# Attention's modulation summed by TensorE, scores two heads ahead, the last tiles by halves, and long matmuls first in the up projections

## The chip, the cores and the metric

One core of one Trainium2 chip. The metric is device time in microseconds (us) of the whole kernel; lower is better.

## The reference, cut to what matters

256 tokens of width 1024 pass through ten phases: attention, an MLP, a recurrent block, an MLP, and then twice a gated feed-forward, a mixer and another gated feed-forward. The change touches the first phase, and one helper that the MLPs and the gated feed-forwards share.

```python
mod = silu(c) @ w + b                      # 1024 x 3072; shift, scale, gate
h = x * (1.0 + scale) + shift
q, k, v = split(h @ w_in)                  # 8 query heads, 2 key and value heads of 128
q, k = partial_rope(q), partial_rope(k)    # the first 32 of 128 are rotated
scores = where(|qpos - kpos| <= 128, q . k * 128**-0.5, -inf)
m = max(max(scores), sink)
probs = exp(scores - m) / (sum(exp(scores - m)) + exp(sink - m))
y = concat(probs @ v) @ w_out
x = layer_norm(2**0.5 * x + (1.0 + gate) * y)
# later: square(relu(h @ w1)) @ w2 (d_ff 4096), and (silu(h @ wg) * (h @ wu)) @ w2 (d_ff 2816)
```

## The kernel before

Weights come as a stream of 128x2048 f32 tiles (1 MB, `raw<-wst`, three slots), each holding two work items in the order of `items_of`. A call of `get` loads up to three tiles ahead on SP's queue and splits items up to four ahead: ScalarE writes the high half `hi` (fp32r, L357), VectorE the low half `lo` = raw - hi (L361). An item in `RAW` or at a phase's head is used unsplit. A product of split operands is three matmuls (hi by hi, low of the activations by hi, high of them by lo): `up_mm` (L385 to L387) and `mv_mm` (L422 to L424). `up_wide`, used by MLPs and feed-forwards alone, puts the first two in one matmul of 512 columns (high and low halves of `hT` side by side, L396) and the third in one of 256 (L397), and alternates the two eight times for one 128-column tile of weights.

Before the phases, the attention's shift and scale are made. `ada0` lies in sixteen chunks of 128x1024 (two halves of eight); VectorE multiplies each by `silu(c)` and adds it up (`mac`, L474 and L476), TensorE sums over partitions with a column of ones (L1560), and ScalarE applies the result to the transposed x (`feature`, L1564, into `hf`); then ScalarE and VectorE split it into `hT` (L374, L376). The two key heads are projected from `hf` unsplit (L411).

Attention (`ph_attn`) then makes v, q of heads 0 and 1, and in a loop over heads: q of head h + 2 with its rotation (`qk`: copy L702, shuffle L704, GpSimd's multiplication L705, VectorE's L706 and L707), the output projection of head h - 2 into four accumulators (two halves of the rows by two halves of the columns, `Down`), the transposes of the probabilities of head h (L737), the scores of h + 1 (L714, with mask, maximum, exponentials and sum in L718 to L729), and the values of h (L746). The last four heads' output tiles are kept back and added in `finish`, half by half, followed by the layer norm (`ln_stats`, L586 to L604), the transposes of x (`turn`, L613) and the first four items of the next phase (L636). Beside this, tasks from the list `side` load and add up the next modulations in VectorE (`aw<-adaw`, L476, closed by `ada_sum`, L490 to L499); `get` takes some of them at each call. A scheduler orders each engine's instructions from this code by dependencies and priorities; every engine, and SP's and GpSimd's DMA queues, then run strictly in that order.

## Time and profile before

| | us |
|---|---|
| median of 3 timed runs | 2131.32 (2127.93 to 2136.0) |
| the profiled execution | 2126.86 |
| its span, first to last instruction | 2125.1 |
| TensorE busy | 2042.1 (96%) |
| VectorE busy | 1568.1 (74%) |
| ScalarE busy | 1112.1 (52%) |
| GpSimd busy | 151.3 (7%) |

The profile is of one execution. An engine's busy time counts the spans of its instructions once; matmuls are pipelined and their ends are modelled, so the rate of matmuls is read from start to start. "Idle before" is the time an engine stood still ahead of an instruction, and the arrow names what ended it. PEclk is the granted share of TensorE's 2.4 GHz.

### The profile page before, as it was taken

To read this page: it belongs to the slowest core of one execution; us is meant where nothing else is said; L and a number is where in the kernel's file an instruction comes from. 1 tells how busy PE (TensorE), PEld (TensorE's weight loads), DVE (VectorE), ACT (ScalarE), POOL (GpSimd) and SP (SyncE) were. 2 spreads that over 40 slices of the span, in tenths; PEclk is the share of its full clock that TensorE was granted. 3 is DMA by queue.
4 is the path that set the end of the run, shared out by engine and by line. 5 is a ranking of instruction groups with operands and counts; after the bars stand their busy time and mean duration, and the time that the engine had idled before them with its cause. 6 is when DMAs were issued, how large, how long until landed. Compare 5 with 4: busy or idle time off the path is not lost.

```text
span 2125.1 us, 33174 instructions
## 1 busy us (share of the span) xinstructions
PE 2042.1 (96%) x13002; PEld 1798.5 (85%) x13002; DVE 1568.1 (74%) x2742; ACT 1112.1 (52%) x1964; POOL 151.3 (7%) x181
## 2 busy tenths in 40 slices
PE   4889999999999999999999999999999999999997
PEld 4778888898888888888999888888889889998886
DVE  5889989987766766689966666676668897667665
ACT  2454455784544555477634355545546774444552
POOL 1210000001010000012011000000001110100000
PEclk8999999999999999999999999999999999999999
DMA  9868884454664555454424465555545344355552
...
DMA packets 67803, 411.67 MB, mean 194 GB/s; under 512 B 8272, under 2 KB 8448, under 8 KB 26944
## 3 DMA queue, kind: packets, MB, share of 16 engines
...
q14 instruction: 53, 0.43, 0.1%
...
## 4 chain that ended last, share of the span: by engine, by line
PE 76%; DVE 13%; DMA 3%; ACT 3%; issue 2%; POOL 2%; POOLq 0%; DVEq 0%; SPq 0%; ACTq 0%
PE pu L396 19%; PE pu L397 10%; PE acc L422 6%; PE acc L423 6%; PE acc L424 6%; PE pu L385 3%; PE hd L636 3%; DVE lo L361 3%; PE pu L387 3%; PE pu L386 3%; DMA raw<-wst 2%; PE py L387 1%; PE py L385 1%; PE py L386 1%; DVE X L589 1%
## 5 line engine op out<-in xcount | busy, mean ns | idle before, releaser
L361 DVE TENSOR_TENSOR lo<-raw,hi 128x1024 fp32r<-128x1024 f32 (+1 forms) x689 | 731.4, 1071 | 313.2 <-ACT hi L357 300.1
L357 ACT ACTIVATE hi<-raw 128x1024 fp32r<-128x1024 f32 x574 | 605.0, 1057 | 548.1 <-PE pu L396 208.2
L396 PE MATMUL pu<-hT,hi 128*128 128x512 f32 x1760 | 625.5, 397 | 0.0
L397 PE MATMUL pu<-hT,lo 128*128 128x256 f32 x1760 | 493.3, 280 | 0.0
L396 PEld LDWEIGHTS pu<-hT,hi 128*128 128x128 f32 x1760 | 330.5, 188 | 80.1 <-ACT tT L374 0.4
L397 PEld LDWEIGHTS pu<-hT,lo 128*128 128x128 f32 x1760 | 332.2, 189 | 5.0
L422 PE MATMUL acc<-hi,tT 128*128 128x512 f32 x688 | 270.7, 395 | 2.3 <-ACT tT L374 2.3
L423 PE MATMUL acc<-hi,tT 128*128 128x512 f32 x688 | 271.1, 394 | 0.6 <-DVE tT L376 0.6
L424 PE MATMUL acc<-lo,tT 128*128 128x512 f32 x688 | 269.7, 392 | 0.0
L385 PE MATMUL pu<-hT,hi 128*128 128x256 f32 x896 | 261.5, 292 | 0.2 <-DVE sp L455 0.2
L387 PE MATMUL pu<-hT,lo 128*128 128x256 f32 x896 | 255.6, 285 | 4.0 <-DVE lo L361 4.0
L386 PE MATMUL pu<-hT,hi 128*128 128x256 f32 x896 | 255.6, 285 | 0.0
L385 PEld LDWEIGHTS pu<-hT,hi 128*128 128x128 f32 x896 | 172.6, 193 | 10.8 <-issue 9.7
L387 PEld LDWEIGHTS pu<-hT,lo 128*128 128x128 f32 x896 | 172.5, 193 | 4.3 <-DVE lo L361 4.2
L386 PEld LDWEIGHTS pu<-hT,hi 128*128 128x128 f32 x896 | 172.6, 193 | 1.2 <-issue 1.0
L422 PEld LDWEIGHTS acc<-hi,tT 128*128 128x128 f32 x688 | 129.0, 188 | 34.3 <-ACT tT L374 4.6
L424 PEld LDWEIGHTS acc<-lo,tT 128*128 128x128 f32 x688 | 129.3, 188 | 28.5 <-DVE lo L361 0.4
L423 PEld LDWEIGHTS acc<-hi,tT 128*128 128x128 f32 x688 | 129.2, 188 | 24.6 <-DVE tT L376 2.7
L636 PE MATMUL hd<-h,raw 128*128 128x128 f32 x960 | 113.2, 277 | 0.1
L636 PEld LDWEIGHTS hd<-h,raw 128*128 128x128 f32 x960 | 110.4, 193 | 2.4 <-ACT h L615 1.5
L405 DVE TENSOR_TENSOR u<-pu,u 128x256 f32<-128x256 f32 x140 | 59.0, 422 | 66.9 <-ACT u L404 66.8
L476 DVE SCALAR_TENSOR_TENSOR aacc<-aw,csil,aacc 128x1024 f32<-128x1024 f32 x70 | 89.3, 1276 | 0.9 <-DMA aw<-adaw 0.8
...
## 6 DMA issues: line engine op xcount, KB each, us to landing
raw<-wst SPq DMA_DIRECT2D x318, 1024.0 KB, 4.9
...
```

The lines of the kernel that those rows point to most:

```text
L357: S.activation(out=hi[:, 0:n], in_=r, func=AF.Copy)
L361: V.tensor_tensor(out=lo[:, c:c + m], in0=r[:, c:c + m], in1=hi[:, c:c + m].bitcast(F32), op=ALU.subtract)
L385: T.matmul(ps, lhsT=hi[:, c], rhs=r[:, 0:256], start=kk == 0, stop=False)
L386: T.matmul(ps, lhsT=hi[:, c], rhs=r[:, 256:512], start=False, stop=False)
L387: T.matmul(ps, lhsT=lo[:, c], rhs=r[:, 0:256], start=False, stop=kk == KT - 1)
L396: T.matmul(ps, lhsT=hi[:, c], rhs=r, start=kk == 0, stop=False)
L397: T.matmul(ps[:, 0:256], lhsT=lo[:, c], rhs=r[:, 0:256], start=False, stop=kk == KT - 1)
L422: T.matmul(ps, lhsT=th, rhs=hi, start=first, stop=False)
L423: T.matmul(ps, lhsT=tl, rhs=hi, start=False, stop=False)
L424: T.matmul(ps, lhsT=th, rhs=lo, start=False, stop=last)
L476: V.scalar_tensor_tensor(out=acc, in0=w, scalar=csil[:, k:k + 1], in1=acc, op0=ALU.mult, op1=ALU.add)
L636: T.matmul(ps[:, half * 128:half * 128 + 128], lhsT=w[:, kk * 128:kk * 128 + 128], rhs=h32[:, kk, :], start=kk == 0, stop=kk == KT - 1)
```

## The change

Modulation: the chunks get six slots of their own. `silu(c)` is spread over 32 columns (`csr`), and each chunk is four matmuls with it, one for each quarter of the chunk's columns, into the four 32-row groups of one PSUM tile (`chunk_mm`). When eight are summed, ScalarE copies the tile, TensorE transposes it in two pieces and VectorE adds the bias (`sums`). The second half's chunks alternate with the key matmuls of the first. The splits into `hT` are written after all keys. On the queues, sinks, mask and rotary table go from GpSimd's to SP's, behind the chunks and three weight tiles.

Attention: q of heads 0 and 1 come before v, the scores of a head two turns ahead of its transposes, the values one turn later. All rotary multiplications are VectorE's, and `nsk` is GpSimd's. The side tasks are to end two items earlier. The last heads' output tiles are added for the first half of the rows before the second.

`up_wide` issues its eight matmuls of 512 columns first and then the eight of 256. `ln_stats` runs through its steps for one half of the columns and then for the other.

```diff
@@ items_of
-        out = [("k", 0), ("k", 1), ("v", 0), ("v", 1), ("q", 0), ("q", 1)]
+        out = [("k", 0), ("k", 1), ("q", 0), ("q", 1), ("v", 0), ("v", 1)]
@@ fused_kernel
-    nc.gpsimd.dma_start(out=vc, in_=vecs.broadcast_to([128, NV]))
...
@@ fetch, get
+    def fetch(n):
+        while ws["dma"] < min(len(st) // 2, n):
             u = ws["dma"]
             raws[u] = pw.tile([128, 2048], F32, tag="raw", bufs=3, name="raw")
             nc.sync.dma_start(out=raws[u], in_=wst[u])
             ws["dma"] += 1
+
+    def get(*key):
+        i = ws["cur"]
+        assert st[i] == key, (st[i], key)
+        fetch(i // 2 + ws["ahead"])
...
-            left = max(1, sum(1 for k in st[i:] if k[0] == key[0]) - (3 if key[0] == "attn" else 20))
+            left = max(1, sum(1 for k in st[i:] if k[0] == key[0]) - (5 if key[0] == "attn" else 20))
@@ up_wide
         hi, lo = w
         for kk in range(KT):
-            c = slice(kk * 128, kk * 128 + 128)
-            r = rhs(kk)
-            T.matmul(ps, lhsT=hi[:, c], rhs=r, start=kk == 0, stop=False)
-            T.matmul(ps[:, 0:256], lhsT=lo[:, c], rhs=r[:, 0:256], start=False, stop=kk == KT - 1)
+            T.matmul(ps, lhsT=hi[:, kk * 128:kk * 128 + 128], rhs=rhs(kk), start=kk == 0, stop=False)
+        for kk in range(KT):
+            T.matmul(ps[:, 0:256], lhsT=lo[:, kk * 128:kk * 128 + 128], rhs=rhs(kk)[:, 0:256], start=False, stop=kk == KT - 1)
 
@@ ln_stats
-        if ln["g1"] is not None:
-            for c, s in enumerate(cs_):
+        for c, s in enumerate(cs_):
+            if ln["g1"] is not None:
                 t = pool.tile([128, 512], F32, tag="t1", bufs=2, name="t1")
                 V.tensor_tensor(out=t, in0=src[c], in1=ln["g1"][:, s], op=ALU.mult)
                 src[c] = t
-        for c, s in enumerate(cs_):
             V.scalar_tensor_tensor(out=X[half][:, s], in0=X[half][:, s], scalar=SQ2, in1=src[c], op0=ALU.mult, op1=ALU.add)
-        for c, s in enumerate(cs_):
             V.bn_stats(out=stt[:, c, :], in_=X[half][:, s])
@@ finish
-                for j, (t, (hi, lo)) in enumerate(tail):
-                    mv_mm(acc[half, c], t, half, hi[:, c * 512:c * 512 + 512], lo[:, c * 512:c * 512 + 512], False, j == n - 1)
+                for j, (t, (hi, lo)) in enumerate(tails[half]):
+                    mv_mm(acc[half, c], t, half, hi[:, c * 512:c * 512 + 512], lo[:, c * 512:c * 512 + 512], False, j == len(tails[half]) - 1)
@@ Down
-                self.tail.append((t, w))
+                for half in range(2):
+                    self.tail[half].append((t, w))
             else:
                 for half in range(2):
-                    for c in range(2):
-                        s = slice(c * 512, c * 512 + 512)
-                        if isinstance(w, tuple):
-                            mv_mm(self.acc[half, c], t, half, w[0][:, s], w[1][:, s], self.k == 0, False)
-                        else:
-                            T.matmul(self.acc[half, c], lhsT=t[:, half * 128:half * 128 + 128], rhs=w[:, s], start=self.k == 0, stop=False)
+                    self.part(half, t, w, self.k == 0)
             self.k += 1
+
+        def part(self, half, t, w, first=False):
+
+            for c in range(2):
+                s = slice(c * 512, c * 512 + 512)
+                mv_mm(self.acc[half, c], t, half, w[0][:, s], w[1][:, s], first, False)
@@ ph_attn
-        V.tensor_scalar(out=nsk, in0=vc[:, 0:8], scalar1=-1.0, scalar2=None, op0=ALU.mult)
-        E1, E2 = G, V
+        G.tensor_scalar(out=nsk, in0=vc[:, 0:8], scalar1=-1.0, scalar2=None, op0=ALU.mult)
...
-            E1.tensor_tensor(out=sw, in0=sw, in1=rp[:, 256:512], op=ALU.mult)
-            E2.tensor_tensor(out=t[0:32, :], in0=t[0:32, :], in1=rp[:, 0:256], op=ALU.mult)
+            V.tensor_tensor(out=sw, in0=sw, in1=rp[:, 256:512], op=ALU.mult)
+            V.tensor_tensor(out=t[0:32, :], in0=t[0:32, :], in1=rp[:, 0:256], op=ALU.mult)
...
-            s = pool.tile([128, 2, 256], F32, tag="s", bufs=2, name="s")
+            s = pool.tile([128, 2, 256], F32, tag="s", bufs=3, name="s")
...
+        for h in range(2):
+            q[h] = qk(("q", h), "q", 4)
+        scores(0)
...
-        for h in range(2):
-            q[h] = qk(("q", h), "q", 4)
+        scores(1)
         ws["side"] = True
-        scores(0)
-        for h in range(8):
-            if h < 6:
-                q[h + 2] = qk(("q", h + 2), "q", 4)
+
+        for h in range(6):
+            q[h + 2] = qk(("q", h + 2), "q", 4)
+            if h >= 1:
+                values(h - 1)
             if h >= 2:
-                dn.add(tT.get(h - 2), get(ph, "o", h - 2))
+                dn.add(tT.pop(h - 2), get(ph, "o", h - 2))
             probs(h)
-            if h < 7:
-                scores(h + 1)
-            values(h)
-            if h == 7:
-                while side:
-                    side.pop(0)()
-                ln_open(ph, nxt)
-        for h in (6, 7):
-            dn.add(tT[h], get(ph, "o", h))
+            scores(h + 2)
+
+        while side:
+            side.pop(0)()
+        values(5)
+        w4 = get(ph, "o", 4)
+        dn.part(0, tT[4], w4)
+        probs(6)
+        w5 = get(ph, "o", 5)
+        dn.part(0, tT[5], w5)
+        ln_open(ph, nxt)
+        values(6)
+        probs(7)
+        w6 = get(ph, "o", 6)
+        values(7)
+        dn.part(1, tT[4], w4)
+        w7 = get(ph, "o", 7)
+        dn.tail = {0: [(tT[6], w6), (tT[7], w7)], 1: [(tT[5], w5), (tT[6], w6), (tT[7], w7)]}
@@ fused_kernel, before the phases
-        nc.gpsimd.dma_start(out=mk, in_=m1)
...
-        nc.gpsimd.dma_start(out=rp, in_=rope)
...
-            acc = [adp.tile([128, D], F32, tag="aacc", bufs=2, name="acc") for _ in range(2)]
+            csr = pool.tile([128, 8, 32], F32, name="csr")
+            V.tensor_copy(out=csr, in_=csil.unsqueeze(2).to_broadcast([128, 8, 32]))
         aws, hps = {}, {}
 
-        def chunks(n, ks=range(8)):
-            for k in ks if mod else ():
-                aws[n, k] = adp.tile([128, D], F32, tag="aw", bufs=4, name="aw")
+        def chunks(n):
+            for k in range(8 if mod else 0):
+                aws[n, k] = pool.tile([128, D], F32, tag="aw", bufs=6, name="aw")
                 nc.sync.dma_start(out=aws[n, k], in_=ada0[n, k])
 
-        def feature(n, f):
-
...
+        def chunk_mm(n, k):
+
+            for j in range(4 if mod else 0):
+                T.matmul(mps[n][32 * j:32 * j + 32, 0:256], lhsT=csr[:, k, :], rhs=aws[n, k][:, j * 256:j * 256 + 256], start=k == 0, stop=k == 7)
+
+        def sums(n):
+
+            if not mod:
+                return
+            quad = pool.tile([128, 256], F32, tag="qd", bufs=2, name="qd")
+            S.activation(out=quad, in_=mps[n][:, 0:256], func=AF.Copy)
+            pt = mps[n][:, 256:512]
+            for b in range(2):
+                T.transpose(pt[:, b * 128:b * 128 + 128], quad[:, b * 128:b * 128 + 128], idn)
+            mc[n] = pool.tile([128, 8], F32, name=f"mc{n}")
+            pairs = lambda t: t.rearrange("p (j b) -> p b j", b=2)
+            V.tensor_tensor(out=pairs(mc[n]), in0=pt.rearrange("p (b j r) -> p b j r", b=2, j=4)[:, :, :, 0], in1=pairs(ab[:, n, :]), op=ALU.add)
+
+        def features(n):
+
+            for f in range(4):
+                src = xps[(n * 4 + f) // 2][:, (n * 4 + f) % 2, :]
+                if mod:
+                    t = hf[n][:, f, :] if hf else pool.tile([128, 256], F32, tag="mt", bufs=8, name="mt")
+                    S.activation(out=t, in_=src, func=AF.Identity, scale=mc[n][:, 4 + f:5 + f], bias=mc[n][:, f:f + 1])
+                    src = t
+                srcs.append(src)
...
-                if n == 0:
-                    hps[j] = (get("attn", "k", j), ps_up("k")[:, 0:256])
-                up_raw(hps[j][0], hps[j][1], range(n * 4, n * 4 + 4))
+                up_raw(hps[j][0], hps[j][1], [kk])
...
-        mps = [ps_up("mc")]
-        for k in range(8 if mod else 0):
-            mac(acc[0], aws[0, k], k)
-        tail = [lambda f=f: feature(0, f) for f in range(4)] + [lambda: keys(0)]
-        chunks(1, range(3))
-        for n, f in enumerate(tail):
-            f()
-            if mod:
-                mac(acc[1], aws[1, n], n)
-            if n == 4:
-                chunks(1, range(5, 8))
-            if n == 2:
-                chunks(1, range(3, 5))
-        mps.append(ps_acc("mc"))
-        for k in range(5, 8 if mod else 0):
-            mac(acc[1], aws[1, k], k)
+        mps = [ps_up("mc") for _ in range(2)]
+        srcs = []
+        for k in range(8):
+            chunk_mm(0, k)
+        chunks(1)
+        if ph0 == "attn":
+            fetch(3)
+            nc.sync.dma_start(out=rp, in_=rope)
+            nc.sync.dma_start(out=mk, in_=m1)
+        nc.sync.dma_start(out=vc, in_=vecs.broadcast_to([128, NV]))
+        sums(0)
+        features(0)
         for f in range(4):
-            feature(1, f)
-        keys(1)
+            keys(f)
+            for k in (2 * f, 2 * f + 1):
+                chunk_mm(1, k)
+        sums(1)
+        features(1)
+        for f in range(4):
+            keys(4 + f)
+        for kk, src in enumerate(srcs):
+            split(hT[:, kk, 0:256], hT[:, kk, 256:512], src)
         ws["ahead"] = 3
```

TensorE before the phases; `mc` is the modulation, `xt` the transposed x, `acc` VectorE's accumulator. Before:

```order
L1583 MATMUL xt<-cs,X_77 128x128
L1560 MATMUL mc<-ones,acc 128x1 x8
L411 MATMUL k<-hf,raw 128x256 x8
L1560 MATMUL mc<-ones,acc 128x1 x4
L411 MATMUL k<-hf,raw 128x256
L1560 MATMUL mc<-ones,acc 128x1 x2
L411 MATMUL k<-hf,raw 128x256 x2
L1560 MATMUL mc<-ones,acc 128x1 x2
L411 MATMUL k<-hf,raw 128x256 x5
L765 MATMUL v<-raw,hf 128x256 x16
```

And now, with `qd` the copied sums:

```order
L1604 MATMUL xt<-cs,X_77 128x128
L1563 MATMUL mc<-aw,csr 32x256 x27
L1573 MATMUL mc<-cs,qd 128x128 x2
L412 MATMUL k<-hf,raw 128x256 x4
L1563 MATMUL mc<-aw,csr 32x256 x4
L412 MATMUL k<-hf,raw 128x256 x3
L1563 MATMUL mc<-aw,csr 32x256 x4
L412 MATMUL k<-hf,raw 128x256
L1563 MATMUL mc<-aw,csr 32x256 x24
L1573 MATMUL mc<-cs,qd 128x128 x2
L412 MATMUL k<-hf,raw 128x256 x8
```

The sums over chunks stand on TensorE, the second half's between the key matmuls, and eight key matmuls are left behind the last chunk as before.

VectorE at a head in the second half of attention: `sw` is the shuffled part of q, `sc` the scores, `sm` their maxima and sums, `tT` the split values. Before:

```order
L727 RECIPROCAL sm<-sm 128x2
L476 SCALAR_TENSOR_TENSOR aacc<-aw,csil,aacc 128x1024
L361 TENSOR_TENSOR lo<-raw,hi 128x1024
L707 TENSOR_TENSOR q<-q,sw 32x256
L704 STREAM_SHUFFLE sw<-q 32x256
L361 TENSOR_TENSOR lo<-raw,hi 128x1024
L706 TENSOR_TENSOR q<-q,rp 32x256
L476 SCALAR_TENSOR_TENSOR aacc<-aw,csil,aacc 128x1024
L707 TENSOR_TENSOR q<-q,sw 32x256
L718 TENSOR_TENSOR sc<-sc,mk 128x256
L376 TENSOR_TENSOR tT<-o,tT 128x256
L721 TENSOR_REDUCE sm<-sc 128x2
```

And now:

```order
L703 STREAM_SHUFFLE sw<-q 32x256
L363 TENSOR_TENSOR lo<-raw,hi 128x1024
L725 TENSOR_TENSOR sm<-sm 128x2
L704 TENSOR_TENSOR sw<-sw,rp 32x256
L726 RECIPROCAL sm<-sm 128x2
L705 TENSOR_TENSOR q<-q,rp 32x256
L378 TENSOR_TENSOR tT<-o,tT 128x256
L706 TENSOR_TENSOR q<-q,sw 32x256
L477 SCALAR_TENSOR_TENSOR aacc<-aw,csil,aacc 128x1024
L363 TENSOR_TENSOR lo<-raw,hi 128x1024
L477 SCALAR_TENSOR_TENSOR aacc<-aw,csil,aacc 128x1024
L717 TENSOR_TENSOR sc<-sc,mk 128x256
```

The rotation is four VectorE instructions behind the shuffle where it was three, and the addition to `sm` stands ahead of the mask of another head's scores.

TensorE at the end of attention, with numbers: accumulators 604 and 605 (now 647 and 648) are the first half of the rows, the other two the second. Before:

```order
L424 MATMUL acc_604<-lo_887,tT_939 128x512
L423 MATMUL acc_605<-hi_886,tT_939 128x512
L424 MATMUL acc_605<-lo_887,tT_939 128x512
L423 MATMUL acc_606<-hi_886,tT_939 128x512
L424 MATMUL acc_606<-lo_887,tT_939 128x512
L423 MATMUL acc_607<-hi_886,tT_939 128x512
L424 MATMUL acc_607<-lo_887,tT_939 128x512
L613 MATMUL pt_1040<-cs_80,X0_76 128x128 x4
L613 MATMUL pt_1049<-cs_80,X0_76 128x128 x4
L636 MATMUL hd_1060<-h32_1039,raw_884 128x128 x2
```

And now:

```order
L423 MATMUL acc_647<-hi_940,tT_994 128x512
L423 MATMUL acc_648<-hi_940,tT_994 128x512
L424 MATMUL acc_647<-hi_940,tT_994 128x512
L425 MATMUL acc_647<-lo_941,tT_994 128x512
L424 MATMUL acc_648<-hi_940,tT_994 128x512
L425 MATMUL acc_648<-lo_941,tT_994 128x512
L425 MATMUL acc_649<-lo_858,tT_935 128x512
L423 MATMUL acc_649<-hi_894,tT_979 128x512
L424 MATMUL acc_649<-hi_894,tT_979 128x512
L425 MATMUL acc_649<-lo_895,tT_979 128x512
L423 MATMUL acc_649<-hi_940,tT_994 128x512
L424 MATMUL acc_649<-hi_940,tT_994 128x512
```

The last head's tile went into all four accumulators directly ahead of the transposes; now it goes into the first two, and sixteen matmuls of the second half, of which six are shown, stand between it and the transposes.

## Rows read from the trace of the kernel before

**Rows 1.** Page, span in 40 slices: busy tenths of TensorE
```profile
PE   4889999999999999999999999999999999999997
```
**Rows 2.** Four stretches: us, busy us and counts per engine, clock, DMA share, GB/s
```profile
0.00:12.50 12.50, 0.00 (x0) 0.02 (x1) 2.43 (x6) 2.98 (x4) 5.32 (x12) 1.00 0.88 318
12.50:46.20 33.70, 19.14 (x80) 15.97 (x80) 24.18 (x34) 7.87 (x17) 0.00 (x0) 0.75 0.94 328
46.20:137.00 90.80, 79.48 (x420) 66.43 (x421) 74.29 (x141) 41.80 (x98) 18.68 (x15) 0.98 0.77 287
137.00:150.00 13.00, 7.71 (x49) 6.95 (x48) 12.54 (x27) 8.09 (x13) 1.60 (x4) 0.87 0.34 136
```
**Rows 3.** Timeline, modulation: start us, us, engine, line, tiles, idle before and releaser
```profile
12.51 3.65 PE L1583 MATMUL xt<-cs,X 128*128 128x128 f32 x16 [12.51 <-DMA cs<-cst]
...
14.64 0.17 DVE L695 TENSOR_SCALAR nsk<-vc 128x8 f32<-128x8 f32 x1 [6.84 <-DMA vc<-vecs]
...
38.36 1.28 DVE L476 SCALAR_TENSOR_TENSOR acc<-aw,csil,acc 128x1024 f32<-128x1024 f32 x1 [0.56 <-DMA aw<-ada]
...
45.78 0.81 ACT L702 ACTIVATE k<-k 128x256 f32<-128x256 f32 x2 [0.34 <-PE k L411]
```
**Rows 4.** Two stretches of modulation, columns as in rows 2
```profile
20.00:30.00 10.00, 4.06 (x16) 3.71 (x16) 5.71 (x11) 3.70 (x8) 0.00 (x0) 0.51 0.97 336
30.00:40.00 10.00, 5.59 (x18) 4.43 (x19) 8.22 (x9) 0.00 (x0) 0.00 (x0) 0.63 0.89 322
```
**Rows 5.** Timeline of TensorE: a column-group sum and its successor; an unsplit projection
```profile
86.53 3.62 PE L411 MATMUL pu<-hf,raw 128*128 128x256 f32 x16
...
200.26 0.64 PE L497 MATMUL ada<-aacc,ones 128*32 128x256 f32 x8
...
200.82 0.50 PE L422 MATMUL acc<-hi,tT 128*128 128x512 f32 x1
```
**Rows 6.** VectorE groups, 46 to 137 us: busy, mean ns of one, idle before
```profile
L476 DVE SCALAR_TENSOR_TENSOR aacc<-aw,csil,aacc 128x1024 f32<-128x1024 f32 x23 | 29.2, 1269 | 0.1
...
L361 DVE TENSOR_TENSOR lo<-raw,hi 128x1024 fp32r<-128x1024 f32 (+1 forms) x20 | 17.5, 895 | 2.5 <-ACT hi L357 2.5
...
L718 DVE TENSOR_TENSOR sc<-sc,mk 128x256 f32<-128x256 f32 x8 | 3.4, 421 | 4.4 <-PE sc L714 4.4
...
L707 DVE TENSOR_TENSOR q<-q,sw 32x256 f32<-32x256 f32 x8 | 3.3, 410 | 5.5 <-POOL sw L705 5.4
...
L726 DVE TENSOR_TENSOR sm<-sm 128x2 f32<-128x2 f32 x8 | 1.7, 216 | 1.7 <-ACT s L725 1.7
```
**Rows 7.** Timeline of GpSimd: one rotary multiplication
```profile
107.35 3.08 POOL L705 TENSOR_TENSOR sw<-sw,rp 32x256 f32<-32x256 f32 x1 [0.95 <-DVE sw L704]
```
**Rows 8.** TensorE group of the transposes of probabilities, 46 to 137 us
```profile
L737 PE MATMUL pt<-cs,s 128*128 128x128 f32 x32 | 6.5, 300 | 6.1 <-ACT s L729 6.1
```
**Rows 9.** Timeline, end of attention: first layer-norm multiplication, first transposes
```profile
136.97 1.28 DVE L586 TENSOR_TENSOR t<-acc,g 128x512 f32<-128x512 f32 x2
...
143.42 1.97 PE L613 MATMUL pt<-cs,X 128*128 128x128 f32 x8 [5.29 <-ACT X L604]
```
**Rows 10.** Timeline of TensorE: narrow run; up tile and long run behind it
```profile
402.51 0.28 PE L386 MATMUL pu<-hT,hi 128*128 128x256 f32 x1
...
410.06 0.28 PE L386 MATMUL pu<-hT,hi 128*128 128x256 f32 x1
...
1454.87 0.40 PE L396 MATMUL pu<-hT,hi 128*128 128x512 f32 x1
...
1455.11 0.28 PE L397 MATMUL pu<-hT,lo 128*128 128x256 f32 x1
...
1457.69 0.40 PE L422 MATMUL acc<-hi,tT 128*128 128x512 f32 x1
...
1460.44 0.39 PE L396 MATMUL pu<-hT,hi 128*128 128x512 f32 x1
```
**Rows 11.** Page, costliest groups: long matmuls of the up projections
```profile
L396 PE MATMUL pu<-hT,hi 128*128 128x512 f32 x1760 | 625.5, 397 | 0.0
```

33 lines of the change are left out of this document (8 added, 25 removed).

## The prediction

> **What bounds the kernel now.** I read the slices of the span first, then the stretches around attention, then who waits there. The slices [rows 1] show TensorE at nine tenths nearly everywhere: outside the first 150 us a change can only win by making its matmuls follow each other faster. The start is different. [rows 2] cut it: nothing on TensorE for 12.5 us, then 33.7 us in which it is busy 19.1, then 90.8 us of attention, and 13 us of layer norm and turn. In the second stretch the DMA engines are 94% busy at 328 GB/s; in the third VectorE is busy 74.3 of 90.8 us, TensorE 79.5 by modelled ends (which overlap), DMA 77%. So: modulation is bound by DMA, attention by VectorE with TensorE waiting in bursts, the rest by TensorE's rate.
>
> **Modulation.** Before, VectorE multiplies sixteen chunks of 512 KB into two accumulators. It first waits 6.84 us for the sinks' broadcast (`nsk`), and the multiplication of the last chunk begins at 38.36, when the chunk has landed; the copy of the first finished key starts at 45.78 [rows 3]. The change gives TensorE the sum. Its price is shown by `ada<-aacc,ones`, the same shape in the same four column groups: four such matmuls, eight records, start at 200.26 and the next work starts at 200.82, so 0.56 us a chunk [rows 5], against 1.5 us for the chunk's DMA. Sixteen chunks are 9 us of TensorE time beside DMA; VectorE loses all sixteen multiplications. What is left is bytes: sixteen chunks (8.4 MB), the first weight tile (1.05), x, constants and rows (1.7) are 11.2 MB. 318 GB/s for 12.5 us bring 4.0, the other 7.2 at 328 GB/s take 22 us [rows 2], so the last chunk lands at about 35 instead of 38.4. The mask, the rotary table and the sinks (0.5 MB) move from GpSimd's queue to SP's, behind the weights of q and v: they come at about 43, and the keys' rotation, their first reader, is not due before 44. SP is held once: the eighth chunk needs the second one's slot, free after the transposes, which wait for the constants until 12.5 and take 3.65 [rows 3]; seven chunks are in flight by then. Then 0.6 us of matmuls, about 1.6 of copy, two transposes and an addition, 0.6 for the first feature, and the last eight key matmuls (sixteen records of about 0.22, as in the 3.62 us of [rows 5]) give 35 + 6.3 = 41.3 for the keys, not 45.8: **-4.5**. The bounds come from the clock. From 20 to 40 us half speed is granted for much of the time [rows 4], since before TensorE is idle after the transposes until the accumulator is ready. Afterwards it has a chunk every 1.5 us, so I take 2.4 GHz. At 1.2 GHz a chunk costs 1.12 and the 32 key records 0.43 each, 18 + 14 us of matmuls after 16.2 and two turns of the sum: keys at about 51, +5. Lower end -7: the 6.84 us wait is the most that the start could give if DMA were no bound.
>
> **Attention.** Two things are taken off VectorE's path. The ten rotary multiplications go from GpSimd to VectorE: ten more of about 0.41 busy (0.33 of them added when they follow each other), +3.3 us. But one of them took GpSimd 3.08 us [rows 7], and VectorE waited 5.5 us for `sw` [rows 6]. Scores two heads ahead take away waits for scores (4.4 us on VectorE [rows 6]) and part of the 6.1 us that TensorE waits for `s` before the probabilities' transposes [rows 8]. They do not shorten VectorE's list: 23 multiplications of the next modulations (29.2 us), 20 subtractions for the low halves (17.5) and so on stay [rows 6]. So VectorE's sum decides: 74.3 + 3.3 = 77.6 us of work. Of the idle 16.5 I keep 8: the wait for `hi` (2.5), and some 5.5 behind the exponentials, the modulation sums and late tiles, now that a reduction and its addition stand closer in three heads. VectorE's list begins with the keys, 4.5 us earlier than at 46.2, less about 1, since its first entry is now the low half of q0, behind ScalarE's splits: 42.6. 42.6 + 77.6 + 8 = 128.2 against 136.97 for the first instruction of the layer norm [rows 9], that is -8.8, of which 4.5 were counted: **-4.3** for the body. DMA allows it: 287 GB/s over 90.8 us are 26 MB, in 86 us 303 GB/s, below the 328 above. Ends: -10 (no idle left but 2.5) and +4 (the waits stay, the moved work is added). What is queued behind new waits: on SP the weight tile of q5 waits for the slot of v, which is now read behind q0, q1 and the first scores, and the modulation chunks behind it on the queue wait too; up to four chunks are in VectorE's hands by then, 4 x 1.27 us of work [rows 6], which about covers it. On VectorE the mask of head 1 now waits for v's matmuls; the four subtractions that q2 and q3 need stand ahead of it.
>
> **The last tiles.** The first half of the rows is finished first, and sixteen long matmuls of the second stand after it. Before, TensorE waits 5.29 us for the normalised X, until 143.42 [rows 9]; afterwards about 3.7 us of that are filled, by work that before lay beside VectorE's, so it moves no end by itself. But the last stretch was granted 0.87 of the clock [rows 2], 3.4 us at 1.2 GHz in the transposes and head matmuls behind the gap; with a gap under 2 us I expect none: **-1.3**, between 0 and -1.7. Layer-norm statistics by halves of the columns: the built order of VectorE is the same as before, 0.
>
> **Up projections.** The 1760 pairs [rows 11] are 220 tiles of eight. One tile, alternating, takes 2.82 us, 1454.87 to 1457.69: 240 ns from a long start to a narrow one, 112 back. The twelve long matmuls behind it take 2.75, or 229 ns each; narrow ones in a row start every 120 ns (63 steps from 402.51 to 410.06) [rows 10]. Eight and eight are 1.833 + 0.960 = 2.793: -0.027 a tile, 220 times **-6**. Both prices are of runs, so I take them. Ends by mixing the rows: long 229 with narrow 112 gives -19, long 240 with narrow 120 gives +13. The low halves are needed later by 1 us, but no wait for them shows at the narrow matmul, so this is no term.
>
> Against this stands the Trainium skill, TensorE: Matmul & The Clock Gate, "Back-to-back issue gap": the gap between matmuls depends on their own columns alone (N/2.4 GHz plus 2.5 ns), so their order would be indifferent. By it this term is 0 and the result 2121 rather than 2115. The trace does not fit that rule (229 and 120 ns, where it has 216 and 109), so I give it a small chance.
>
> **Sum.** -4.5 - 4.3 - 1.3 - 6 = -16 from the profiled execution's own 2126.9, or 2111. That execution is 4.4 below the median of the runs shown (2131.3), so 2115 is the forecast for a median.
>
> **The rivals.**
> 1. Order is indifferent: up projections 0, the rest as above, 2131 - 10 = 2121. For it: both orders load the same weights and stream the same columns. Against it: 2.82 against 2.793 in rows.
> 2. VectorE gives nothing back: the waits for scores and tables are replaced by waits for exponentials and chunks, and the moved multiplications cost their 3.3 us. -4.5 + 3.3 - 1.3 - 6 = -8.5: 2123. For it: VectorE already has 82% there. Against it: 5.5 us of its idle time have GpSimd's name on them.
> 3. Slower: runs of narrow matmuls do not cover their weight loads. Alternating, a long one stands on either side of every narrow one; in a run the load for the next has only a narrow one to lie behind, so narrow ones cost their 120 ns, and if the long ones gain nothing and stay at 240, a tile costs 2.88: +0.06 x 220 = +13, with -10 elsewhere 2134. It decides from 2.865 a tile on, where it eats the rest. Against it: 229 ns for long ones in a row.
> 4. The modulation runs at 1.2 GHz: +5 instead of -4.5, and VectorE starts as late; 2131 - 6 = 2125.
> 5. The body closes nearly all gaps (-10): 2109.
>
> **How the numbers follow.** Forecast 0.50, rivals 0.17, 0.15, 0.05, 0.07, 0.06. A measurement of this kernel can tell about 0.5%, 10.7 us, so faster means below 2120.6. The forecast's own terms spread by some 6 us, so five sixths of it are below, all of rival 5, half of rival 1, a third of rival 2 and a quarter of 4: 0.64 faster; slower by over 0.5% needs rival 3 with the rest failing too: 0.03; 0.33 the same. The range goes from below rival 5, which also takes in a third of the way to the -19 of the up projections, 2102, to above rivals 2 and 4, 2127.
>
> **What would show it.** Last chunk's matmuls at 35 to 36 and key copies at 41 to 43, with full clock from 17 us on; `sw` on VectorE and no wait for it; the first layer-norm multiplication at 126 to 131; no granted half clock at the turn; eight long matmuls at 229 and eight narrow at 120 in every up tile, 2.79 us. I am wrong if the keys come after 46, if VectorE idles over 12 us in attention, or if a tile takes 2.82 or more.

## The result, and the profile after

Four timed runs of the changed kernel have a median of 2110.43 us (2109.36 to 2112.29), four of the kernel before 2132.94. The ratio is 0.9895, with a 95% interval of 0.9874 to 0.9915: faster by 1.05%, which is clear of the 0.5% that a measurement can tell. Between the two profiled executions the difference is smaller, 2126.86 to 2112.29, or 14.6 us; the experiments come back to the 8 us that lie between.

The same four stretches as in [rows 2], in the changed kernel (us; busy us and counts of TensorE, its weight loads, VectorE, ScalarE, GpSimd; granted clock, DMA share, GB/s):

```profile
0.00:12.50 12.50, 1.91 (x10) 0.50 (x10) 0.67 (x5) 2.98 (x4) 3.25 (x9) 1.00 0.85 328
12.50:43.40 30.90, 23.88 (x172) 14.26 (x173) 4.42 (x11) 8.37 (x20) 0.98 (x1) 0.89 0.96 361
43.40:133.00 89.60, 81.05 (x409) 68.20 (x408) 74.97 (x150) 39.42 (x97) 4.13 (x5) 0.92 0.80 290
133.00:146.00 13.00, 10.51 (x58) 9.05 (x57) 12.27 (x26) 5.78 (x9) 1.60 (x4) 0.87 0.11 28
```

The modulation ends 2.8 us earlier, with DMA busy for 0.96 of it, and VectorE has 4.42 us of work in it where it had 24.18. The attention between them is hardly shorter, 89.6 us against 90.8, with as much VectorE work as before and a lower clock, 0.92 against 0.98. The timelines of TensorE, ScalarE and VectorE answer [rows 3, 9] (start, us, engine, line, tiles, idle before and its releaser):

```profile
34.73 0.96 PE L1563 MATMUL mc<-aw,csr 128*32 128x256 f32 x8 [0.63 <-DMA aw<-ada]
...
37.79 5.65 PE L412 MATMUL k<-hf,raw 128*128 128x256 f32 x16 [0.93 <-ACT hf L1584]
```
```profile
43.04 0.82 ACT L701 ACTIVATE k<-k 128x256 f32<-128x256 f32 x2 [1.78 <-PE k L412]
```
```profile
132.97 1.29 DVE L587 TENSOR_TENSOR t<-acc,g 128x512 f32<-128x512 f32 x2
```
```profile
139.51 1.39 PE L612 MATMUL pt<-cs,X 128*128 128x128 f32 x8 [2.44 <-ACT X L603]
```

The last chunk is multiplied at 34.73, the first key is copied at 43.04 (45.78 before), the first layer-norm product comes at 132.97 (136.97), the first transposes of the turn at 139.51 (143.42). So 3.9 us are won by the turn. The other 10.7 lie behind it. From start to start, the 3520 matmuls of the up projections take 613.1 us where they took 619.5: 6.4 us are won in the tiles themselves, and 4.3 elsewhere behind the turn. One tile, from TensorE's timeline, and the group of its long matmuls on the page (busy us, mean ns), to be read beside [rows 10, 11]:

```profile
1443.53 2.00 PE L396 MATMUL pu<-hT,hi 128*128 128x512 f32 x8
1445.37 1.12 PE L398 MATMUL pu<-hT,lo 128*128 128x256 f32 x8
1446.32 0.40 PE L423 MATMUL acc<-hi,tT 128*128 128x512 f32 x1
```
```profile
L396 PE MATMUL pu<-hT,hi 128*128 128x512 f32 x1760 | 439.0, 391 | 0.0
```

Eight long matmuls take 1.84 us and eight narrow ones 0.95, together 2.79 where the tile of [rows 10] took 2.82. (The group's fall from 625.5 to 439.0 us is no time won: in turn with narrow ones, the modelled span of a long matmul also covered most of the narrow one behind it.)

### The profile page after: what moved, and what is told of

Its sections match the earlier page's. It is cut to its first block, busy times and chain, and to the rows that moved or that the text cites. A ratio compares the mean times of both kernels' runs of the same rounds, so it can differ in the third digit from the quotient of the medians.

```text
span 2110.5 us, 33323 instructions
## 1 busy us (share of the span) xinstructions
PE 2044.7 (97%) x13102; PEld 1802.8 (85%) x13102; DVE 1551.4 (74%) x2730; ACT 1101.9 (52%) x1966; POOL 136.6 (6%) x169
## 4 chain that ended last, share of the span: by engine, by line
PE 80%; DVE 11%; issue 3%; ACT 3%; DMA 2%; POOL 2%; POOLq 0%; DVEq 0%; SPq 0%; ACTq 0%
PE pu L396 19%; PE pu L398 10%; PE acc L424 7%; PE acc L423 7%; PE acc L425 7%; PE hd L635 3%; PE pu L387 3%; PE pu L389 3%; PE pu L388 3%; DVE lo L363 3%; PE py L389 1%; PE py L387 1%; PE py L388 1%; DVE X L589 1%; DVE stt L590 1%
## 5 line engine op out<-in xcount | busy, mean ns | idle before, releaser
L396 PE MATMUL pu<-hT,hi 128*128 128x512 f32 x1760 | 439.0, 391 | 0.0
L389 PE MATMUL pu<-hT,lo 128*128 128x256 f32 x896 | 256.5, 286 | 4.6 <-DVE lo L363 4.6
L398 PEld LDWEIGHTS pu<-hT,lo 128*128 128x128 f32 x1760 | 240.1, 190 | 17.2
L398 PE MATMUL pu<-hT,lo 128*128 128x256 f32 x1760 | 245.4, 282 | 0.0
L376 ACT ACTIVATE tT<-r 128x256 fp32r<-128x256 f32 x152 | 63.3, 416 | 237.3 <-DVE r L841 135.8
L389 PEld LDWEIGHTS pu<-hT,lo 128*128 128x128 f32 x896 | 173.2, 193 | 5.0 <-DVE lo L363 5.0
L378 DVE TENSOR_TENSOR tT<-r,tT 128x256 fp32r<-128x256 f32 x152 | 64.4, 424 | 58.7 <-ACT tT L376 58.7
```

The costliest lines, as they stand in the source:

```text
L378: (eng or V).tensor_tensor(out=dlo, in0=src, in1=dhi.bitcast(F32), op=ALU.subtract)
L389: T.matmul(ps, lhsT=lo[:, c], rhs=r[:, 0:256], start=False, stop=kk == KT - 1)
L396: T.matmul(ps, lhsT=hi[:, kk * 128:kk * 128 + 128], rhs=rhs(kk), start=kk == 0, stop=False)
L398: T.matmul(ps[:, 0:256], lhsT=lo[:, kk * 128:kk * 128 + 128], rhs=rhs(kk)[:, 0:256], start=False, stop=kk == KT - 1)
```

## The experiments

Three marks cut the start of every run: the copy of the first key, the first layer-norm product and the first transposes of the turn. "Body" is the second minus the first. All of them are read from each run's own trace. Four kernels have the same attention (changed, e5, e2, e6): their bodies lie within 0.4 us of each other, 89.6 to 89.9. Some of the expectations count the turn from the first head matmul behind these transposes instead, 1.2 to 1.8 us later: 145.2 in the kernel before, 140.7 and 139.1 in the changed kernel's two traces. Medians can be set against each other among e1 to e4, e5 to e8 and e9 to e11, which were timed together; elsewhere the ratio to the kernel before is the measure.

| kernel | key copy | body | turn | profiled, us | median, us (runs) |
|---|---|---|---|---|---|
| before | 45.78 | 91.19 | 143.42 | 2126.86 | 2131 to 2135 in each group |
| e1, up order alone | 45.92 | 92.11 | 144.48 | 2126.63 | 2121.81 (9) |
| e9, moved product alone | 45.49 | 85.70 | 137.74 | 2120.32 | 2125.16 (7) |
| e3, modulation alone | 42.98 | 97.81 | 148.28 | 2137.41 | 2133.00 (12) |
| e10, modulation and product | 41.70 | 86.28 | 134.51 | 2121.57 | 2124.69 (7) |
| e12, e10 and up order | 42.97 | 84.80 | 134.30 | 2111.49 | 2113.66 (6) |
| changed | 43.04 | 89.93 | 139.51 | 2112.29 | 2110.43 (4) |
| e5, changed again | 41.60 | 89.59 | 137.73 | 2111.16 | 2111.16 (5) |
| e2, changed without up order | 41.44 | 89.58 | 137.54 | 2123.47 | 2125.09 (9) |
| e7, last tiles whole | 43.21 | 87.47 | 137.22 | 2110.66 | 2110.91 (4) |
| e6, extra matmuls | 41.86 | 89.67 | 138.06 | 2110.99 | 2110.92 (4) |
| e8, product back on GpSimd | 40.51 | 110.46 | 157.49 | 2139.57 | 2139.52 (10) |
| e4, weights on GpSimd's queue | 41.21 | 85.33 | 133.07 | 2111.81 | 2117.00 (6) |
| e11, multiply sooner | 42.12 | 88.44 | 138.68 | 2121.70 | 2120.88 (6) |

**The order of the up projections, done alone (e1) and undone alone (e2).**

```diff
-            T.matmul(ps, lhsT=hi[:, c], rhs=r, start=kk == 0, stop=False)
-            T.matmul(ps[:, 0:256], lhsT=lo[:, c], rhs=r[:, 0:256], start=False, stop=kk == KT - 1)
+            T.matmul(ps, lhsT=hi[:, kk * 128:kk * 128 + 128], rhs=rhs(kk), start=kk == 0, stop=False)
+        for kk in range(KT):
+            T.matmul(ps[:, 0:256], lhsT=lo[:, kk * 128:kk * 128 + 128], rhs=rhs(kk)[:, 0:256], start=False, stop=kk == KT - 1)
```

> The kernel before with nothing but the long matmuls of an up projection ahead of its narrow ones. Theory (the reorder is worth what the cadences of the two traces say, 2.786 against 2.817 us a tile on 220 tiles): 6 to 8 us under the kernel before, up tiles at 2.78 to 2.79 us, the first layer-norm product still at 137 us, mlp0's clock as before. Rival (the order is worth more, since the medians of the two kernels lie 22 us apart and the traces 15): 11 us or more. Second rival (order indifferent, the shorter tile of the changed kernel comes from elsewhere): within 2 us of the kernel before.

> The changed kernel with long and narrow matmuls of an up projection in turn again, as before; modulation, attention and last tiles stay changed. Theory: the tiles go back to 2.82 us, and 7 to 9 us are left of the gain over the kernel before, all of it won by the end of mlp0's first tiles. Rival (the start and the attention hold more than the two traces show): 13 us or more are left. Second rival (nothing but the order counts): within 3 us of the kernel before.

e1 against the kernel before: 0.9951 (0.9935 to 0.9967), about 10 us. e2: 0.9960 (0.9947 to 0.9973), 8.5 us left. In e1's trace the tile is that of the changed kernel:

```profile
1453.44 2.00 PE L394 MATMUL pu<-hT,hi 128*128 128x512 f32 x8
1455.28 1.12 PE L396 MATMUL pu<-hT,lo 128*128 128x256 f32 x8
1456.23 0.40 PE L421 MATMUL acc<-hi,tT 128*128 128x512 f32 x1
```

In e2's trace a long matmul is followed after 235 ns on average (1760 pairs), as in the kernel before. So the order sets the tile, and the second rival falls. But e1's gain is nearer to 11 than to the 6 to 8 of the tiles, while its profiled execution, 2126.63, is no faster than that of the kernel before. The second of these comes from the clock. Stretches of e1 and, for the same work, of the changed kernel (columns as above):

```profile
1070.00:1080.00 10.00, 10.00 (x144) 9.72 (x145) 4.33 (x6) 2.03 (x4) 2.62 (x2) 1.00 0.10 42
1080.00:1090.20 10.20, 10.20 (x62) 9.52 (x61) 2.50 (x3) 3.25 (x6) 0.52 (x1) 0.50 0.30 105
1779.90:1789.90 10.00, 9.93 (x144) 9.49 (x142) 4.59 (x6) 2.57 (x5) 3.24 (x2) 1.00 0.18 75
1789.90:1800.10 10.20, 10.20 (x65) 9.45 (x63) 2.88 (x3) 2.33 (x6) 0.53 (x1) 0.50 0.29 103
```
```profile
1064.20:1074.20 10.00, 10.00 (x144) 9.72 (x145) 4.34 (x6) 1.99 (x4) 2.58 (x2) 1.00 0.10 42
1074.20:1084.40 10.20, 10.20 (x102) 9.80 (x102) 4.38 (x6) 4.95 (x9) 0.53 (x1) 1.00 0.27 104
```

TensorE does the same 144 matmuls without a gap; then it is granted 1.2 GHz for 10.2 us in e1, and 2.4 GHz in the changed kernel. The two places lie in the two mixers. From the transposes ahead of a mixer to those behind it, e1 takes 332.5 and 332.4 us where the changed kernel takes 328.4 and 328.1: 4.1 and 4.3 us. Without them e1's span would be 8.6 us below that of the kernel before, although its turn is 1.1 us later. The tiles give 6.4 of it; another 3 us come behind the turn, outside the tiles. Undoing the order (e2) shows the same: without its one stretch, e2 takes some 9 us more from the turn to the end than the changed kernel, 6.3 of them in the tiles.

**The changed kernel, timed again (e5).** No edit.

> The changed kernel itself, timed again. Theory (the gain is the 15 us between the two traces; the medians lie 22 us apart because stretches of 10 us at half clock at about 1080 and 1790 us, with TensorE fully busy, come in some runs of the kernel before and by chance in none of the four runs of the changed one): the times now spread from 2109 to 2120 us, median 2112 to 2117, mean granted clock 0.985 to 0.99. Rival (the change itself keeps the clock up in these places): all times within 2 us of 2110.4 again, at a clock of 0.990.

Five runs: 2109.39 to 2114.78 us, median 2111.16, ratio 0.9906 (0.9887 to 0.9924). Three are within 2 us of 2110.4 and two, at a mean clock of 0.988, lie 4 us above, about one such stretch. So neither expectation holds in full: the changed kernel is probably not free of them, but has few. Of the fourteen traces of this study e1 and e3 show both stretches and e2, e8, e10 and e11 one; the changed kernel's two traces and that of the kernel before show none. That a profiled execution of the kernel before without them (2126.86) is set against timed runs that often have them is the likely source of most of the 8 us between the two comparisons. Timed runs leave no trace, but they do leave a mean clock. Of the 62 timed runs of the kernel before that go with the experiments, the 15 at 0.990 or more average 2129.0 us, the 20 at 0.986 or less 2135.8; the nine of the changed kernel all lie at 0.988 to 0.991. That fits, but where the clock fell in these runs is not shown. What decides whether the clock falls there stays open.

**The moved rotary product: back on GpSimd in the changed kernel (e8), and moved alone in the kernel before (e9).**

```diff
-            V.tensor_tensor(out=sw, in0=sw, in1=rp[:, 256:512], op=ALU.mult)
+            G.tensor_tensor(out=sw, in0=sw, in1=rp[:, 256:512], op=ALU.mult)
```
```diff
-        E1, E2 = G, V
+        E1, E2 = V, V
```

> The changed kernel with one of the three rotary operations back on GpSimd, as before. Theory (on GpSimd the rotary product stands behind the row broadcast and an idle time of 7 to 10 us that follows it, and TensorE waits for that query): one query's product comes 5 us or more late, the first layer-norm product at 136 to 141 us instead of 133, and 3 to 7 us are lost by the turn. Rival (VectorE is the bound, and 0.4 us a head off it is a gain): first layer-norm product at 130 to 132 us, time equal or up to 3 us shorter. Second rival (hidden anyway): within 1 us at the turn.

> The kernel before with the one rotary product that ran on GpSimd put on VectorE, nothing else. Theory (GpSimd stands idle for 7.2 us behind the row broadcast at 97 us, and a query waits there, in the kernel before too): the turn starts 3 to 7 us earlier than at 145.2 us, and the time falls by as much. Rival A (in the old order other work of TensorE covers that wait, it only bites when the scores go two heads ahead): within 1 us at the turn. Rival B (VectorE is the bound, and ten products of 0.4 us on it cost): the turn 1 to 4 us later.

e8 is 28 us slower than the changed kernel, and slower than the kernel before (1.0031, 1.0015 to 1.0046). e9 alone is worth 0.9960 (0.9941 to 0.9979), and the turn starts 5.7 us earlier. The cause is seen in GpSimd's timelines, first in the kernel before (the row right ahead of [rows 7] is its third), then in e8:

```profile
95.34 2.43 POOL L528 PARTITION_BROADCAST g<-arow  x4 [9.32 <-DVE q L706]
97.60 0.89 POOL L510 DMA_DIRECT2D abr<-rows  x1
105.69 0.71 POOL L705 TENSOR_TENSOR sw<-sw,rp 32x256 f32<-32x256 f32 x1 [7.19 <-issue]
```
```profile
88.59 3.91 POOL L529 PARTITION_BROADCAST g<-arow  x3 [9.38 <-DMA aw<-adaw]
105.06 0.71 POOL L704 TENSOR_TENSOR sw<-sw,rp 32x256 f32<-32x256 f32 x1 [12.56 <-issue]
111.80 1.05 POOL L529 PARTITION_BROADCAST g<-arow  x1 [6.03 <-issue]
112.70 0.89 POOL L511 DMA_DIRECT2D abr<-rows  x1
124.17 0.71 POOL L704 TENSOR_TENSOR sw<-sw,rp 32x256 f32<-32x256 f32 x1 [10.58 <-issue]
```

When GpSimd goes from the row broadcast to a product, or from there back to the broadcast in e8, it stands still for 6 to 12.6 us in which it waits for nothing that the profile shows. (Ahead of the first broadcast it is idle for 9.3 us too, but there the profile names a releaser.) The DMA that GpSimd issues in between is not the reason: no issue stands beside the gaps of 12.56 and 6.03. In the built programs an extra instruction stands at each of these changes, and ahead of the first such work; its name there is `PseudoReloadLibraryIndex`, with index 1 ahead of a broadcast and 0 ahead of elementwise work. It is the bare `ISA` in e8's GpSimd:

```
L529 ISA
L529 ISA g_966<-arow 128x256 x3
L704 ISA
L704 TENSOR_TENSOR sw<-sw,rp 32x256
L529 ISA
L529 ISA g_966<-arow 128x256
```

The Trainium skill, GPSIMD Engine Reference, "Terminology", says that GpSimd has kernel libraries which are loaded at run time by DMA. That fits the name, but no run here shows what the extra instruction does. What it costs is shown: in e8 TensorE waits twice for a query behind it, ahead of the scores of heads 5 and 6:

```profile
106.27 2.07 PE L713 MATMUL sc<-k,q 128*128 128x256 f32 x4 [13.32 <-DVE q L706]
...
125.38 2.08 PE L713 MATMUL sc<-k,q 128*128 128x256 f32 x4 [7.99 <-DVE q L706]
```

So e8's turn comes 18 us late, far more than the 3 to 7 that its theory said. On VectorE, the moved product costs less than its own time. The bodies of the kernel before and of e9, then VectorE's multiplications of the queries in the two, and the moved products:

```profile
45.78:136.97 91.19, 79.85 (x422) 66.41 (x421) 74.41 (x142) 42.15 (x99) 18.68 (x15) 0.98 0.77 287
45.49:131.19 85.70, 80.01 (x422) 66.98 (x421) 74.91 (x152) 42.62 (x99) 6.38 (x5) 0.96 0.83 308
```
```profile
L706 DVE TENSOR_TENSOR q<-q,rp 32x256 f32<-32x256 f32 x8 | 4.8, 597 | 0.0
```
```profile
L705 DVE TENSOR_TENSOR sw<-sw,rp 32x256 f32<-32x256 f32 x10 | 4.3, 429 | 0.0
...
L706 DVE TENSOR_TENSOR q<-q,rp 32x256 f32<-32x256 f32 x8 | 3.2, 404 | 0.0
```

Ten more instructions add 0.5 us to VectorE's 74.4. In the kernel before, three of the eight L706 take 0.90 to 0.95 us, each beside a product that runs on GpSimd, and the others 0.40 to 0.41, some of these beside one too; in e9, where none runs there, all eight take 0.39 to 0.41.

**The new modulation alone (e3), and with the moved product (e10).** e3 is the kernel before with the changed start: chunks multiplied by TensorE in column groups, six chunk buffers, angles, masks and vectors on SyncE's queue, `nsk` on GpSimd. e10 is e3 with e9's line.

```diff
-        for k in range(8 if mod else 0):
-            mac(acc[0], aws[0, k], k)
+        for k in range(8):
+            chunk_mm(0, k)
...
```

> The kernel before with the new modulation (column groups, six chunk buffers, the loads of masks, angles and vectors on SyncE's queue behind the chunks, the negated sinks on GpSimd) and the old order in the attention. Theory: key copies at 43 against 45.8 us, and since the attention behind it is held by the order of VectorE's work, 1 to 3.5 us of it reach the end. Rival A (VectorE sets the end of the attention, and takes back all of it): within 1 us of the kernel before. Rival B (the attention's new order only pays together with this start): slower than the kernel before by over 1 us, because the old order then waits for angles and masks that land later.

> The kernel before with the new modulation, and the rotary product on VectorE, in the old order of heads. Theory (the new modulation alone was worth nothing only because the keys came earlier to an attention that GpSimd's idle time held): the turn 3 to 6 us earlier than in the kernel before, 139 to 142 us against 145.2, and the rest of the attention's change is worth at most 1 to 2 us. Rival (the order of heads, two ahead, is what turns the earlier keys into time): the turn at 144 to 147 us, time within 3 us of the kernel before.

e3: 0.9995 (0.9978 to 1.0011), nothing, though its keys come 2.8 us earlier. GpSimd stands still for 10.58 us behind its broadcast, and the query behind it comes so late that the turn starts at 148.28. e10: 0.9954 (0.9933 to 0.9975). Its turn at 134.51 is 3.2 us before e9's, as its keys are 3.8 us earlier; but its median is e9's (2124.69 and 2125.16), and its trace has one 10.2 us stretch at half clock. So the new modulation moves the turn once GpSimd is out of the way, and by the medians and ratios its part in the end is 0 to 2 us. The turn is earlier than the theory said (136.3 by its own mark, where it had 139 to 142), and earlier than in the changed kernel: what else the change does to the attention loses there.

**The attention's order: old heads with everything else that counts (e12), weights on another queue (e4), sooner multiplications (e11), last tiles whole (e7).** e12 is e10 with e1's lines. In e4 the tile weights from q2 on leave SyncE's queue:

```diff
-            nc.sync.dma_start(out=raws[u], in_=wst[u])
+            (nc.gpsimd if ws["pool"] else nc.sync).dma_start(out=raws[u], in_=wst[u])
...
```

In e11 the attention's side tasks multiply two tasks behind the load, not three:

```diff
-                if 0 <= n - 3 < len(seq):
-                    ada_mac(*seq[n - 3])
+                if 0 <= n - lag < len(seq):
+                    ada_mac(*seq[n - lag])
...
```

In e7 both halves of all four last tiles stay in the closing part:

```diff
-        w4 = get(ph, "o", 4)
-        dn.part(0, tT[4], w4)
+        dn.add(tT.pop(4), get(ph, "o", 4))
...
```

> The kernel before with three parts of the change (new modulation, all rotary products on VectorE, long matmuls first) and without the rest: heads one score ahead, last tiles whole, the query weights behind the values, in the order of before. Theory (scores two heads ahead cost 3 to 4 us at the turn, since the run with the new modulation and the moved product in the old order turned at 136.3 us against 139.1 to 140.7): the turn at 135 to 138 us, 2105 to 2109 us in the end, 2 to 5 us under the changed kernel. Rival (what comes earlier at the turn is given back in the recurrent layer behind mlp0, at half clock, as in the run with the weights on GpSimd's queue): the turn at 135 to 138, the layer norm after the recurrent layer at 501 to 503 us against 501.7 and 503.2, and the time within 1.5 us of 2111. It is slower than the changed kernel if stretches at half clock near 1080 and 1790 us come in most of its runs.

> The changed kernel with the weights of the attention's tiles from q2 on issued on GpSimd's queue in place of SyncE's, where each stands behind side-task loads that wait for VectorE's multiplications. Theory (the stall at 107 us is a late weight: q7's load was issued only at 100.9 us and landed at about 108.4, behind a load that waited for a buffer): q7's weights land 4 us or more earlier, the last scores come at 115 to 119 instead of 122.3, and the time falls by 2 to 6 us against the changed kernel, to 2104 to 2108. Rival (VectorE's backlog alone sets the pace, the sum's matmuls ahead of q7 wait for it as before): within 1 us of the changed kernel. It is slower if weights and side loads then take each other's bandwidth.

> The changed kernel with each side-task multiplication of the attention two tasks behind its load instead of three, so that a load waits for a buffer that was given up one task earlier, and SyncE's queue, where the tile weights stand behind these loads, is held less. Theory (q7's weights come late because their issue stands behind a load that waits for VectorE): q7's weights are issued 3 us or more before 100.9 us, the turn starts 2 to 5 us earlier, at 134 to 138 us against 139.1 and 140.7 of the changed kernel's two traces, and the time falls by 1 to 4 us. Rival (the multiplications then wait for loads that have not landed): the turn no earlier, VectorE idle for loads by 3 us or more.

> The changed kernel with the attention's last four output tiles added for both row halves in the closing part, as before, instead of the first half's tiles 4 and 5 earlier. Theory (the halves only move work, the turn still waits for the first half's layer norm at half clock): first turned block 139 to 141 us against 139.5, second at 146 to 147, time within 2 us. Rival (the prediction's: the split saves about 1.3 us by giving TensorE work at the turn): turn later by 1 to 2 us with a longer gap before it.

Where the new order loses is seen in the changed kernel's TensorE at 105 us, and, in the second fence, at the same place in e4:

```profile
105.00 1.02 PE L713 MATMUL sc<-k,q 128*128 128x256 f32 x4
...
109.82 3.44 PE L491 MATMUL ada<-ones,aacc 128*128 128x1 f32 x16 [2.40 <-DVE aacc L477]
113.13 5.52 PE L412 MATMUL pu<-hf,raw 128*128 128x256 f32 x16
...
122.33 1.03 PE L713 MATMUL sc<-k,q 128*128 128x256 f32 x4
```
```profile
104.53 1.88 PE L491 MATMUL ada<-ones,aacc 128*128 128x1 f32 x16
106.27 3.70 PE L412 MATMUL pu<-hf,raw 128*128 128x256 f32 x16
...
114.85 1.03 PE L713 MATMUL sc<-k,q 128*128 128x256 f32 x4
```

In the changed kernel a modulation sum (L491) stands ahead of q7's projection and waits for a side multiplication of VectorE. TensorE idles 2.40 us, runs matmuls of a single column for 3.4, and is granted 1.2 GHz from 110.0 to 116.8, so that q7's sixteen records take 5.52 us instead of 3.70. In e4 it waits for nothing there. Bodies and clocks go together; the windows from key copy to first layer-norm product are, in the order changed, e5, e4, e12:

```profile
43.04:132.97 89.93, 81.38 (x410) 68.49 (x409) 74.94 (x149) 39.78 (x97) 4.13 (x5) 0.92 0.80 290
```
```profile
41.60:131.19 89.59, 81.01 (x410) 68.19 (x409) 74.83 (x149) 40.00 (x97) 4.39 (x6) 0.92 0.80 300
```
```profile
41.21:126.54 85.33, 77.20 (x415) 66.17 (x413) 77.50 (x155) 40.32 (x97) 7.31 (x11) 0.96 0.88 323
```
```profile
42.97:127.77 84.80, 79.32 (x423) 65.76 (x422) 76.86 (x153) 41.76 (x98) 5.28 (x5) 0.98 0.82 301
```

Of the kernels with the product on VectorE, those with a clock of 0.92 take 89.6 to 89.9 us for the body, with 0.94 88.4 and 89.7 (e11, e6), with 0.96 85.3 to 87.5 (e4, e7, e9, e10), with 0.98 84.8. (Part of a lower clock comes from the waits: above, it falls behind the 2.40 us.) So the new order did not shorten the attention: with the product on VectorE, the old one is 3.3 to 5.1 us shorter (e10 and e12 against changed and e5). Not all of that is the scores two heads ahead. With the last tiles whole, the new order's body is 87.47 (e7), so the split tiles make 2.1 to 2.5 us of it, and 1.2 to 2.7 are left for the rest. And with its weights on another queue (e4) the new order is as short as the old. e12's theory of the turn holds, 136.06 by its own mark. Its theory of the end does not: the first matmuls behind the recurrent layer's norm start at 500.5 us (501.7 and 503.2 in the changed kernel), and the median is 2113.66, ratio 0.9924 (0.9898 to 0.9950). e4 ends alike: the last scores come 7.5 us earlier and the turn at 133.07, its profiled execution takes 2111.81, its median 2117.00 (0.9921, 0.9899 to 0.9944). From the turn to the end e4 and e12 need 1976.9 and 1975.5 us, the changed kernel 1971.0 and 1971.7, and 2 to 4 of these 4 to 6 us fall in mlp0 and in the recurrent layer behind it, where the clock falls in other places from one kernel to the next. Why an earlier turn is given back is not settled. No version here beat the changed kernel.

e11 is 0.9930 (0.9909 to 0.9951) against the kernel before, by the ratios some 5 to 7 us slower than the changed one. q7's weights were issued at 103.67 instead of 100.90, so the edit did not do what it was made for; its trace has one of the 10.2 us stretches. That SyncE's queue makes q7 late is therefore shown by e4 alone, and e4 does not tell the late weight from the late sum ahead of it. In e7 the turn starts at 137.22, 94.0 us behind its key copy, where the four kernels with the changed attention need 96.1 to 96.5: finishing the first half's tiles early makes the turn some 2 us later, not earlier. In the median it is nothing (2110.91).

**The clock in the modulation (e6).**

```diff
+                for j in range(6 if 2 <= k < 7 else 0):
+                    again(k, j)
...
```

> The changed kernel with extra matmuls on chunks that have landed, six behind each of the second half's chunks 2 to 6 and eight behind the last, into a bank that nothing reads any more: they fill the 1 us that TensorE waits for the next chunk. Theory (the granted clock falls at 34.9 us because TensorE has little work, and that costs the last key records): full clock through the keys, key copies at 41 to 41.8 us instead of 43.0, and the attention's end 1 to 2 us earlier. Rival A (the clock falls whatever TensorE does, or the extra matmuls are themselves in the way): key copies at 43 us or later. Rival B (the keys come earlier, but VectorE's backlog takes it back): key copies at 41.5, the first layer-norm product still at 132 to 134 us. The time moves by less than 3 us in all cases.

Two stretches of the modulation, the changed kernel's last 6.8 us, then the end of e6's:

```profile
34.90:41.70 6.80, 5.39 (x19) 3.48 (x12) 2.00 (x6) 4.48 (x10) 0.05 (x1) 0.50 0.95 351
```
```profile
26.60:41.86 15.26, 15.17 (x166) 9.33 (x158) 1.60 (x5) 4.36 (x10) 0.21 (x1) 1.00 0.99 366
```

With TensorE busy 15.17 of 15.26 us the clock holds to the keys, whose last sixteen records take 3.72 us instead of 5.65. The copy comes at 41.86, 1.2 us before the changed kernel's and 0.3 behind e5's: in e5, without extra work, half clock fell earlier. The first layer-norm product follows at 131.53, and the median, 2110.92, is unchanged. This does not settle what holds the clock: the kernels that share this start without extra work differ as much. From the end of the transposes to the key copy the mean clock is 1.00 in e8, 0.87 in the changed kernel and 0.81 in e7, and the copies are at 40.51, 43.04 and 43.21; in e2, e4, e5, e10 and e11, where 6.8 us at half clock come in two pieces, at 41.2 to 42.1.

## Why the prediction was right, and where it was wrong

The forecast was 2115 us by a fall of 16 from the profiled execution; that execution fell by 14.6, and the median is 2110.4. The direction and the size are right, but of the four terms one is right, one is right in part, and two are not. As measured, the terms add up to 10.3 (tiles 6.4, keys 2.7, body 1.3, turn -0.1). The other 4.3 us came behind the turn, where the sum has nothing: 1.2 of them are a wait of 1.60 us ahead of the transposes behind the second MLP, which is 0.35 to 0.44 in all thirteen other traces, so an accident of that one execution of the kernel before; what made the rest is open. That the total came so near is in part luck.

- **Up projections, -6.** Right. 2.793 us a tile was forecast from runs of each kind in the trace before; 2.79 was measured, in e1 alone too, and 6.4 us in all 220. Order is not indifferent (rival 1) for these matmuls: 235 ns behind a long one in turn with narrow ones, 229 in a row. The Trainium skill, TensorE: Matmul & The Clock Gate, "Back-to-back issue gap", gives N/2.4 plus 2.5 ns for an isolated matmul, and says that in a stream of weight loads and matmuls both set the spacing. These matmuls are such a stream, so the prediction took the formula further than the page does; the trace has 229 and 120 ns where the formula has 216 and 109. Rival 3 (narrow runs cost) fell: 120 ns, as taken.
- **Modulation, -4.5 at the keys.** -2.7 in the changed kernel, -4.2 in e5, -5.3 in e8. The bytes were right: the last chunk was expected at about 35 and its matmuls start at 34.73. The step that failed is "a chunk every 1.5 us, so I take 2.4 GHz". In the changed kernel TensorE waits 0.6 to 0.7 us for each of the last chunks, which come 1.3 us apart, and half speed was granted from 34.9, over the last key records. At full clock (e8) the term is larger than forecast. Rival 4 named the cause, with a price far too large, since half clock lasted 6.8 us and not the whole stretch.
- **Attention's body, -4.3.** -1.3 and -1.6, and from two parts with opposite signs. The moved product gives -5.5 (e9, body 85.70 against 91.19), as the 5.5 us of waiting in [rows 6] said, and the +3.3 us for the moved work measured +0.5. The reading of [rows 7] was wrong: 3.5 of the 5.5 us of waiting come not from the 3.08 us of one product but from the 7.19 us ahead of the one before it, and that would have grown with the new order (e8: +20 us). The waits credited to scores two heads ahead came back as others. "Of the idle 16.5 I keep 8" is the step that failed: VectorE idles 14.6 us, above the 12 that the prediction itself named as a sign of being wrong, and its groups from 43.4 to 133 us (busy, mean ns, idle before) name 11.9 of them: exponentials, the sum that TensorE had queued behind VectorE's own multiplication, late query copies and late tiles.

```profile
L378 DVE TENSOR_TENSOR tT<-o,tT 128x256 fp32r<-128x256 f32 x8 | 3.3, 414 | 2.3 <-ACT tT L376 2.2
...
L725 DVE TENSOR_TENSOR sm<-sm 128x2 f32<-128x2 f32 x8 | 1.2, 155 | 4.2 <-ACT s L724 4.2
...
L493 DVE SCALAR_TENSOR_TENSOR acol<-ada,cr 128x8 f32<-128x8 f32 x2 | 0.3, 156 | 2.9 <-PE ada L491 2.9
...
L703 DVE LOAD_MASK_SELECT sw<-q x8 | 0.1, 10 | 2.5 <-ACT q L701 2.5
```

  And the sum was made of VectorE's work alone; the clock, 0.92 where it was 0.98, did not stand in it.
- **Last tiles, -1.3.** Nothing. A gap of 2.44 us is left at the turn, 1.2 GHz was granted from 140.7 to 144.1, 3.4 us as before, where none was expected, and e7 shows the split as a cost of some 2 us at the turn. The reordered statistics are 0, as said.
- **From the trace to the median.** 4.4 us were added, because the profiled execution of the kernel before lies that much below its median. The changed kernel's lies 0 to 2 us above its own. That sets the forecast 4 us too high, and it is most of what is missing. (In the chances, the parts of "faster" add up to 0.63 and not 0.64.)

What the runs make of the sum: the order of the up projections and the moved product are worth some 8 to 12 us each by medians and ratios (e1, e9), together with the new modulation 2113.66 (e12); the new order of the heads and the split tiles add nothing that can be told.
